# Expert gate and up weights: eight consecutive feature rows on a partition, and a gather that reads the normed rows with a stride of eight

## Chip, cores and metric

The kernel runs on one core of a Trainium2 chip. The metric is device time in microseconds (us), the median of several executions. A profile of one further execution gives the span from its first to its last instruction, the engines' busy times and the DMA packets. Engines are named as in the profile: PE (matrix multiply, with its weight loads as PEld), DVE (VectorE), ACT (ScalarE), POOL (GpSimd) and SP (SyncE, which here only issues DMAs; its queue is SPq).

## What is computed

A hybrid layer (attention, pooling mixer, gated feed-forward) is followed by two layers that each end in a mixture of experts. All is in 32-bit floats, on 256 tokens of 1024 features. The part that the change touches, per layer `l`:

```python
x = layer_norm(ALPHA * x + mix, ln1_g[l], ln1_b[l])
# grouped_moe: 16 experts, 4 groups, the 2 best experts of the best group per token
hg = jnp.einsum('nd,edf->nef', xt, w_gate)     # w_gate[l]: 16 x 1024 x 512
hu = jnp.einsum('nd,edf->nef', xt, w_up)       # w_up[l]:   16 x 1024 x 512
act = jax.nn.silu(hg) * hu * gates[:, :, None]
out = jnp.einsum('nef,efd->nd', act, w_down)   # w_down[l]: 16 x 512 x 1024
x = layer_norm(ALPHA * x + out, ln2_g[l], ln2_b[l])
```

## The kernel before, in words

Program order per engine is fixed when the kernel is built; engines wait for each other and for DMAs through semaphores. All weights are streamed from HBM by DMAs that SP issues in the order of the text, each as soon as the buffer that it fills is free.

**Attention part of a layer** (lines 802 to 1083): projections, index scores, two kinds of attention, output projection. Towards its end `ex.pump(12)` and `ex.pump(20)` let SP issue the first expert weights.

**Norm and routing** (lines 1085 to 1162): `z` is the normed row tile without scale and shift: tokens on partitions, features as 8 chunks of 128, in two halves `tt` of 128 tokens. `transpose_rows` turns `z` to features on partitions, and `affine` (line 1093) applies the layer norm's scale and shift, which lie per partition in `vec`. POOL splits `z` into `zh` and `zl` (lines 1128 to 1130), two reduced-precision floats that add up to it. The router then gives every token a slot (of 64) in each of its experts.

**Experts** (`routed_experts`, line 1265): 16 experts are taken as 8 pairs `p`. For every four experts `gather(q)` (line 1175) multiplies the rows with a 0/1 slot matrix `G`: for each feature chunk `k` and both halves, `zh` and `zl` are the stationary operand (128 x 128, loaded by a PEld instruction) and `G` the moving one (256 columns). That is 32 matmuls for each `q`, 4 gathers a layer, 256 matmuls in all. ACT (line 1096) or DVE (line 1098) applies `affine` and writes the chunk to `xg`. `gate_up(p, m)` (line 1191) multiplies 64 gathered slots per expert, as the stationary operand, with the gate (m = 0) or up (m = 1) weights: 8 chunks `k` for 2 experts `e`, which stand side by side in PE's columns. Then come silu and product, `slot_rows`, four transposes `pact` (line 1299; the stationary operand is `sg[:, k:512:4]`, every fourth column), `down` and `combine`, which adds the rows back to the tokens.

**Expert weights** (`Experts.pump`, line 722): gate and up weights of an expert come as two halves `h` of four 128-row chunks, `"(k p) f -> p k f"`: chunk `k` has feature row 128 k + p on partition p, so one partition's run in HBM is one row of 512 floats, 2 KB. Down weights come as `"(p k) f -> p k f"`: two rows of 1024 floats that are consecutive, 8 KB in one run. Pair 0's gate weights and the pairs 6 and 7 are loaded in smaller pieces (lines 728 to 738 and 754 to 759); the last pair's down weights in half rows, 2 KB (line 753). `KINDS` says which pool a piece's buffer is from; the pools are shared with activations.

The function `dense_experts` and the branch `need > 64` are a fallback for crowded experts that these inputs don't take.

Of the kernel before, what the change touches and what calls it, by code (L numbers as in the profile page):

```python
# [10 lines left out]
F32 = mybir.dt.float32  # L11
# [9 lines left out]
D = 1024  # L21
KD = D // 128
# [12 lines left out]
def body(tc, a, out, dbg=None, upto=None):  # L35
    nc = tc.nc
    te, ve, se, ge, sy = nc.tensor, nc.vector, nc.scalar, nc.gpsimd, nc.sync
    ctx = ExitStack()
    const = ctx.enter_context(tc.tile_pool(name="const", bufs=1))
# [5 lines left out]
    def A(name, shape=(128, 512)):  # L45

        return psum.tile(list(shape), F32, tag="A", name=name, bufs=4)

    def H(name, shape=(128, 2, 512)):

        return psum.tile(list(shape), F32, tag="H", name=name, bufs=2)

    def act(name, dt=F32, shape=(128, KD, T)):
        return wp.tile(list(shape), dt, tag="act", name=name, bufs=10)
# [18 lines left out]
    def mm(o, l, r, start, stop):  # L73
        return te.matmul(o, lhsT=l, rhs=r, start=start, stop=stop, skip_group_check=True)  # L74
# [26 lines left out]
    def keep_warm(n, dst):  # L101

        for _ in range(n):
            te.transpose(dst, ident, ident)
# [64 lines left out]
    for c in range(4):  # L169
        for u in range(4):  # L170
            if c == u == 0:
                t = W["in00"] = ring.tile([128, 2, 1024], F32, name="in00")
# [13 lines left out]
    for c in range(NF // 2):  # L186
        for s in range(2):
            c0 = s * DFF + 256 * c
# [64 lines left out]
    def V(n, j):  # L253
        b, o = VO[n]
        i = v0[b] + o + j
        if CV[0] <= i < CV[1]:
            return at.conv[:, i - CV[0]:i - CV[0] + 1]
        i -= CV[1] - CV[0] if i >= CV[1] else 0
        return vec[:, i:i + 1]

    def cload(name, shape, src, dt=F32, eng=None):
        t = const.tile(list(shape), dt, name=name)
        (eng or ge).dma_start(t, src)
        return t
# [19 lines left out]
    upb = cload("upb", (128, 2, 128), a["c_up"], BF16)  # L284
    cr = cload("cr", (128, 100), a["c_route"])
    iota64, tri, gsum = cr[:, 0:64], cr[:, 68:84], cr[:, 84:100]
    rbias = cload("rbias", (128, 16), a["router_bias_2"].partition_broadcast(128))

    rw = const.tile([128, (KD + 1) * 16], F32, name="rw")
# [368 lines left out]
    for i in range(NF):  # L658
        if True:
            ps = up_pair(i)  # L660
# [23 lines left out]
    ovf = const.tile([128, 2], F32, name="ovf")  # L684
    flag = const.tile([1, 1], I32, name="flag")
    m8 = const.tile([128, 2, 8], F32, name="m8")
    R = const.tile([128, 11, 32], F32, name="R")
    selb = const.tile([128, 2, 16], BF16, name="selb")
    gcol = const.tile([128, 8], F32, name="gcol")
    rn = const.tile([128, 4, 4], F32, name="rn")  # L690
# [21 lines left out]
    class Experts:  # L712
# [9 lines left out]
        def pump(self, n):  # L722
            while self.n < min(n, len(self.todo)):
                p, m, h, e = self.todo[self.n]
                shape = [128, 4, 512] if m < 2 else [128, 2, D]
                kind = KINDS[self.n]
                name = f"e{self.l}{p}{m}{h}{e}"
                if p == m == 0:

                    self.n += 2  # L730
                    for b in range(2):
                        for e in range(2):
                            t = ring.tile([128, 2, 512], F32, name=name)
                            c0 = 512 * h + 256 * b
                            sy.dma_start(t, a["w_gate_2"][self.l, e, c0:c0 + 256].rearrange("(k p) f -> p k f", p=128))
                            for k in range(2):
                                W[f"e{self.l}00{h}{e}", 2 * b + k] = t[:, k]
                    continue
                if kind == "r":
                    t = ring.tile(shape, F32, name=name)  # L740
                else:
                    t = dict(a=act, h=hl8, p=pp8)[kind](name, F32, shape)
                src = a[("w_gate_2", "w_up_2", "w_down_2")[m]][self.l, 2 * p + e]
                src = src.rearrange("(k p) f -> p k f" if m < 2 else "(p k) f -> p k f", p=128)[:, shape[1] * h:shape[1] * (h + 1)]
                if p < 6:
                    sy.dma_start(t, src)
                elif p == 7 and m == 2:

                    self.final.append((t, src))
                    if len(self.final) == 4:  # L750
                        for c in range(2):
                            for t_, s_ in self.final:
                                sy.dma_start(t_[:, :, 512 * c:512 * c + 512], s_[:, :, 512 * c:512 * c + 512])
                elif e:

                    for i in range(2):
                        s = slice(i * shape[1] // 2, (i + 1) * shape[1] // 2)
                        for t_, s_ in (self.last, (t, src)):
                            sy.dma_start(t_[:, s], s_[:, s])
                self.last = t, src  # L760
                for k in range(shape[1]):
                    W[name, k] = t[:, k]
                self.n += 1

    def transpose_rows(z, evac, one_bank):

        n = 2 if one_bank else 4
        pt = [A("pt", (128, 2, T)) if one_bank else H("pt", (128, 4, T)) for _ in range(KD // n)]
        if one_bank:
            keep_warm(36, pt[3][:, 1, 0:128])  # L770
        for tt, k in [(tt, k) for k in range(KD) for tt in range(2)] if one_bank else [(tt, k) for tt in range(2) for k in range(KD)]:
            if not one_bank and tt == 1 and k == 0:
                keep_warm(8, pt[1][:, 3, 128:])
            te.transpose(pt[k // n][:, k % n, tt * 128:(tt + 1) * 128], z(k, tt), ident)
        for k in range(KD):
            evac(k, pt[k // n][:, k % n])
# [22 lines left out]
    def layer(l, xT, xh, xl, general=False):  # L799
# [285 lines left out]
        z = act("z", shape=(128, 2, KD, 128))  # L1085
        zh, zl = act("zh", F32R, (128, 2, KD, 128)), act("zl", F32R, (128, 2, KD, 128))
# [3 lines left out]
                normalise(z[:, tt, 4 * c:4 * c + 4], acc[tt][c].rearrange("t (k p) -> t k p", p=128), mv, (se, ve)[c])  # L1090
        xp = act("xp")

        def affine(dst, src, k, eng):
            g, b = V(f"ln1g{l}", k), V(f"ln1b{l}", k)
            if eng is se:
                se.activation(dst, src, AF.Identity, scale=g, bias=b)
            else:
                ve.tensor_scalar(dst, src, g, b, op0=ALU.mult, op1=ALU.add)  # L1098

        transpose_rows(lambda k, tt: z[:, tt, k], lambda k, ps: affine(xp[:, k], ps, k, (se, ve)[k // 4]), False)  # L1100
        se.activation(warm[:, 0:1], xp[0:1, 3, 0:1], AF.Sigmoid)
        if dbg is not None and upto == f"xp{l}":
            sy.dma_start(dbg, xp)
# [19 lines left out]
        def rv(i):  # L1123
            return R[:, i].rearrange("p (t e) -> p t e", t=2)

# [5 lines left out]
        ve.tensor_tensor(out=bia, in0=aff, in1=rbias[:, None, :].to_broadcast([128, 2, 16]), op=ALU.add)  # L1131
        b4 = R[:, 1].rearrange("p (g e) -> p g e", e=4)
        cmp = t1("cmp", (128, 2, 8, 4, 4))
# [7 lines left out]
                             in1=tri[:, None, :].to_broadcast([128, n, 16]), op=ALU.is_gt)  # L1141
            ve.tensor_reduce(out=out, in_=o, axis=AX.X, op=ALU.add)

        rank, two = (R[:, i].rearrange("p (g e) -> p g e", e=4) for i in (10, 5))
        rank4(rank, b4, 8, 0)

        ve.scalar_tensor_tensor(out=two, in0=rank, scalar=1.5, in1=b4, op0=ALU.is_lt, op1=ALU.mult)
        q8 = [R[:, 9, 8 * i:8 * i + 8] for i in range(3)]
        ve.tensor_reduce(out=q8[0], in_=two, axis=AX.X, op=ALU.add)
        rank4(q8[1].rearrange("p (t g) -> p t g", t=2), q8[0].rearrange("p (t g) -> p t g", t=2), 2, 0)  # L1150
        ve.tensor_scalar(q8[2], q8[1], 0.5, None, op0=ALU.is_lt)
# [15 lines left out]
        def slots(q):  # L1167

            G = t2("G", (128, 2, 256), F32R)
            for tt in range(2):  # L1170
                ve.tensor_tensor(out=G[:, tt].rearrange("p (e s) -> p e s", s=64), in0=iota64[:, None, :].to_broadcast([128, 4, 64]),
                                 in1=sid[:, tt, 4 * q:4 * q + 4, None].to_broadcast([128, 4, 64]), op=ALU.is_equal)
            GS[q] = G

        def gather(q, bs=range(4)):

            G = GS[q]
            if q not in XG:
                XG[q] = act("xg", shape=(128, KD, 256))
            xg = XG[q]  # L1180
            for b in bs:
                pg = A("pg", (128, 2, 256))
                for tt in range(2):
                    for i in range(2):
                        k = 2 * b + i
                        mm(pg[:, i], zh[:, tt, k], G[:, tt], tt == i == 0, False)
                        mm(pg[:, i], zl[:, tt, k], G[:, tt], False, tt == 1)
                for i in range(2):
                    affine(xg[:, 2 * b + i], pg[:, i], 2 * b + i, (se, ve)[b % 2])

        def gate_up(p, m):
            ps = A("gu")
# [66 lines left out]
        def gates_():  # L1259
            ve.scalar_tensor_tensor(out=gat, in0=sid, scalar=0.5, in1=aff, op0=ALU.is_gt, op1=ALU.mult)  # L1260
            ve.tensor_reduce(out=R[:, 7, 2:4], in_=gat, axis=AX.X, op=ALU.add)
            ve.reciprocal(R[:, 7, 4:6], R[:, 7, 2:4])
            ve.scalar_tensor_tensor(out=gat, in0=gat, scalar=1 / ALPHA, in1=R[:, 7, 4:6, None].to_broadcast([128, 2, 16]), op0=ALU.mult, op1=ALU.mult)
# [88 lines left out]
        for tt in range(2):  # L1352
# [6 lines left out]
            for c in range(2):  # L1359
                s = slice(c * 512, c * 512 + 512)  # L1360
                v, g, b = z2[:, tt, s], gb[:, 0, s], gb[:, 1, s]
# [130 lines left out]
```

## Time and profile before

| | us |
|---|---|
| median of 3 executions (1076.24 to 1078.51) | 1077.11 |
| the profiled execution's own time | 1077.54 |
| its span, first to last instruction | 1075.8 |
| PE busy | 1026.4 (95%) |
| DVE busy | 540.2 (50%) |
| ACT busy | 428.1 (40%) |
| POOL busy | 88.6 (8%) |
| DMA, mean of 16 engines | 295.08 MB at 274 GB/s |

Busy times overlap, and a busy PE is not PE at its peak. The profiled execution's time is 1.7 us over its span and 0.4 us over the median of the others. The expert stages lie at 488 to 706 us (first of the two layers) and 844 to 1067 us (second).

### The profile page before, as it was taken

The page shows a single profiled execution, that of the slowest core. Times are in us where ns is not written, and L with a number is a line of the kernel's source. Part 1 is how long each engine was busy: PE and PEld are TensorE (multiplying, and loading weights), DVE is VectorE, ACT ScalarE, POOL GpSimd, SP SyncE. Part 2 cuts the span into 40 slices and gives each one's busy share as a digit, 9 for nine tenths or more (in the row PEclk, how much of TensorE's full clock was granted, in tenths as well). Part 3 has the DMA queues.
Part 4 walks back from the last instruction along what each step waited for, and adds up shares of the span by engine and source line. Part 5 has one row for each costly group of instructions (what it writes and reads, how often), then busy time and mean ns, then how long its engine had stood idle before and what let it go on. Part 6 is the DMA issues. An engine that isn't in the chain of part 4 may idle for free.

```text
span 1075.8 us, 16369 instructions
## 1 busy us (share of the span) xinstructions
PE 1026.4 (95%) x6620; PEld 729.0 (68%) x6620; DVE 540.2 (50%) x1022; ACT 428.1 (40%) x795; POOL 88.6 (8%) x88
## 2 busy tenths in 40 slices
PE   9999999999999999998999999989999899999995
PEld 7889999999999999764343434378976534343432
DVE  6775668977776789653010111058985302021103
ACT  5675548655554565541010111166654302011111
POOL 3400021000000120020000000043000200000001
PEclk9999999999999999999999999999999899999998
DMA  9943555755443254987999999964297899999994
GB/s 341 349 141 130 169 197 195 245 187 196 132 130 143 84 196 158 340 309 263 398 396 393 395 399 395 378 225 175 90 345 276 299 374 393 400 399 400 395 387 155
DMA packets 131636, 295.08 MB, mean 274 GB/s; under 512 B 6022, under 2 KB 34896, under 8 KB 125280
## 3 DMA queue, kind: packets, MB, share of 16 engines
q1 hardware_dynamic: 129936, 290.44, 73.5%
q0 software_dynamic: 1312, 2.97, 0.8%
q8 instruction: 54, 0.88, 0.3%
q10 hardware_dynamic: 304, 0.53, 0.1%
q14 instruction: 30, 0.25, 0.1%
HBM read 291.82 MB, written 2.10 MB: 273 GB/s over the span
## 4 chain that ended last, share of the span: by engine, by line
PE 75%; DVE 13%; DMA 6%; ACT 5%; issue 1%; SPq 0%; POOL 0%; ACTq 0%; DVEq 0%; POOLq 0%
PE gu L74 20%; PE up L74 12%; PE pd L74 8%; PE fm L74 7%; PE yT L74 5%; PE tm L74 4%; PE sc L74 4%; DVE hl L86 3%; PE prj L74 3%; PE pg L74 3%; PE wo L74 2%; PE sum L74 2%; DMA e<-in_w_up_dram 2%; DMA e<-in_w_down_dram 1%; ACT P L399 1%
## 5 line engine op out<-in xcount | busy, mean ns | idle before, releaser
L74 PE MATMUL gu<-e,xg 128*64 128x512 f32 x1024 | 228.1, 597 | 1.3 <-ACT sg L1284 1.3
L74 PEld LDWEIGHTS gu<-e,xg 128*64 128x64 f32 x1024 | 71.6, 138 | 135.4 <-issue 128.0
L74 PE MATMUL up<-h2h,hl 128*128 128x256 f32 x704 | 130.5, 283 | 0.0
L74 PE MATMUL pd<-e,aT 128*64 128x512 f32 x512 | 113.8, 596 | 2.4 <-ACT aT L1301 2.3
L74 PEld LDWEIGHTS up<-h2h,hl 128*128 128x128 f32 x704 | 111.4, 192 | 0.0
L74 PE MATMUL up<-h2l,hl 128*128 128x256 f32 x352 | 99.7, 283 | 0.1
L74 PEld LDWEIGHTS pd<-e,aT 128*64 128x64 f32 x512 | 35.2, 137 | 72.0 <-issue 64.7
L74 PEld LDWEIGHTS up<-h2l,hl 128*128 128x128 f32 x352 | 67.6, 192 | 0.3 <-DVE h2l L524 0.3
L1215 DVE TENSOR_REDUCE gcol<-pgt 64x1 f32<-64x2 f32 x32 | 5.0, 157 | 124.8 <-PE pgt L74 124.5
L1290 DVE SCALAR_TENSOR_TENSOR sg<-gu,gcol,sg 128x512 f32<-128x512 f32 x16 | 12.0, 751 | 110.1 <-PE gu L74 110.1
L74 PE MATMUL yT<-ac,hl 128*128 128x256 f32 x528 | 67.0, 283 | 0.1
L74 PEld LDWEIGHTS yT<-ac,hl 128*128 128x128 f32 x528 | 64.9, 192 | 0.3 <-ACT ac L644 0.3
L86 DVE TENSOR_TENSOR hl<-up,hl 128x1024 fp32r<-128x1024 f32 x44 | 53.8, 1225 | 19.5 <-ACT hl L96 19.4
L1284 ACT ACTIVATE sg<-gu 128x512 f32<-128x512 f32 x16 | 9.6, 598 | 128.0 <-PE gu L74 128.0
L96 ACT ACTIVATE hl<-up 128x1024 fp32r<-128x1024 f32 x44 | 46.1, 1051 | 33.9 <-PE up L74 28.4
L1316 ACT ACTIVATE y<-pd 128x512 fp32r<-128x512 f32 x32 | 18.5, 597 | 99.5 <-PE pd L74 80.7
L86 DVE TENSOR_TENSOR y<-pd,y 128x512 fp32r<-128x512 f32 x32 | 21.3, 686 | 66.4 <-ACT y L1316 66.4
L1301 ACT ACTIVATE aT<-pact 128x512 f32<-128x512 f32 x16 | 9.6, 599 | 110.4 <-PE pact L1299 110.4
L74 PE MATMUL fm<-hh,hl 128*128 128x256 f32 x256 | 49.2, 288 | 0.9 <-ACT vu L325 0.9
L1098 DVE TENSOR_SCALAR xg<-pg,vec 128x256 f32<-128x256 f32 x32 | 15.9, 538 | 61.2 <-PE pg L74 39.3
L86 DVE TENSOR_TENSOR hl<-in,hl 128x1024 fp32r<-128x1024 f32 x32 | 38.6, 1220 | 11.2 <-ACT hl L96 10.9
L74 PE MATMUL prj<-xhn,hl 128*128 128x256 f32 x208 | 40.3, 288 | 3.9 <-DVE iq L86 2.7
(357 smaller groups left out, 2073.2 us busy)
## 6 DMA issues: line engine op xcount, KB each, us to landing
e<-in_w_up_dram SPq DMA_DIRECT2D x48, 1024.0 KB, 14.1
e<-in_w_down_dram SPq DMA_DIRECT2D x48, 1024.0 KB, 13.6
e<-in_w_gate_dram SPq DMA_DIRECT2D x40, 1024.0 KB, 14.5
e<-in_w_gate_dram SPq DMA_DIRECT2D x48, 512.0 KB, 10.6
up<-in_w_up_dram SPq DMA_DIRECT2D x22, 1024.0 KB, 5.1
e<-in_w_up_dram SPq DMA_DIRECT2D x32, 512.0 KB, 10.8
e<-in_w_down_dram SPq DMA_DIRECT2D x32, 512.0 KB, 10.7
in<-in_w_in_dram SPq DMA_DIRECT2D x15, 1024.0 KB, 15.9
```

The costliest lines, as they stand in the source:

```text
L74: return te.matmul(o, lhsT=l, rhs=r, start=start, stop=stop, skip_group_check=True)
L86: return (eng or ve).tensor_tensor(out=dst, in0=src, in1=hi.bitcast(F32), op=ALU.subtract)
L96: se.activation(hi, raw, AF.Copy, scale=scale)
L399: se.activation(P[:, i, c:c + n], S[:, i, c:c + n], AF.Exp, scale=scale if isinstance(scale, float) else scale[:, tt:tt + 1], bias=m[:, 1, ...
L1098: ve.tensor_scalar(dst, src, g, b, op0=ALU.mult, op1=ALU.add)
L1215: ve.tensor_reduce(out=gcol[r, p:p + 1], in_=pt[r, x:x + 17:16], axis=AX.X, op=ALU.add)
L1284: se.activation(sg, psg, AF.Silu)
L1290: ve.scalar_tensor_tensor(out=sg, in0=psu, scalar=gcol[:, p:p + 1], in1=sg, op0=ALU.mult, op1=ALU.mult)
L1301: se.activation(aT, pt, AF.Copy)
L1316: se.activation(h_, pd[c], AF.Copy)
```

## The change

Feature row 8 p + k, in place of 128 k + p, now lies on partition p in chunk k, for gate and up weights alike. So four consecutive rows (8 KB) of one partition are one run in HBM; pieces of two rows are runs of 4 KB. The sum over features is the same in another order, and the gathered rows have to follow: `gather` takes every eighth feature from column k on as its stationary operand (a step of 32 bytes), and `affine` takes scale and shift from a new tile `lnp` that holds them in the same order, loaded by four small DMAs on POOL's queue early in the program. `R` shrinks by three planes, whose contents move to free ones. The down weights and the fallback stay.

```diff
+    lnp = const.tile([128, 2, 2, KD], F32, name="lnp")
+    for l in range(2):
+        for i, n in enumerate(("ln1_g_2", "ln1_b_2")):
+            ge.dma_start(lnp[:, l, i], a[n][l].rearrange("(p k) -> p k", k=KD))
...
-    R = const.tile([128, 11, 32], F32, name="R")
+    R = const.tile([128, 8, 32], F32, name="R")
...
-                            c0 = 512 * h + 256 * b
-                            sy.dma_start(t, a["w_gate_2"][self.l, e, c0:c0 + 256].rearrange("(k p) f -> p k f", p=128))
+                            src = a["w_gate_2"][self.l, e].rearrange("(p k) f -> p k f", p=128)
+                            sy.dma_start(t, src[:, 4 * h + 2 * b:4 * h + 2 * b + 2])
...
-                src = src.rearrange("(k p) f -> p k f" if m < 2 else "(p k) f -> p k f", p=128)[:, shape[1] * h:shape[1] * (h + 1)]
+                src = src.rearrange("(p k) f -> p k f", p=128)[:, shape[1] * h:shape[1] * (h + 1)]
...
-        def affine(dst, src, k, eng):
-            g, b = V(f"ln1g{l}", k), V(f"ln1b{l}", k)
+        def affine(dst, src, g, b, eng):
...
-        rank, two = (R[:, i].rearrange("p (g e) -> p g e", e=4) for i in (10, 5))
+        rank, two = (R[:, i].rearrange("p (g e) -> p g e", e=4) for i in (2, 5))
...
-        q8 = [R[:, 9, 8 * i:8 * i + 8] for i in range(3)]
+        q8 = [R[:, 6, 8 * i:8 * i + 8] for i in range(3)]
...
+            zf = [[v[:, tt].rearrange("p k c -> p (k c)") for v in (zh, zl)] for tt in range(2)]
...
-                        mm(pg[:, i], zh[:, tt, k], G[:, tt], tt == i == 0, False)
-                        mm(pg[:, i], zl[:, tt, k], G[:, tt], False, tt == 1)
+                        mm(pg[:, i], zf[tt][0][:, k:D:KD], G[:, tt], tt == i == 0, False)
+                        mm(pg[:, i], zf[tt][1][:, k:D:KD], G[:, tt], False, tt == 1)
...
-                    affine(xg[:, 2 * b + i], pg[:, i], 2 * b + i, (se, ve)[b % 2])
+                    k = 2 * b + i
+                    affine(xg[:, k], pg[:, i], lnp[:, l, 0, k:k + 1], lnp[:, l, 1, k:k + 1], (se, ve)[b % 2])
```

On PE, DVE, ACT and SP the instructions stand in the same order as before, with the same sizes. On POOL four DMAs are added, in the program's opening, between the routing constants and the router's bias. Before:

```order
L263 DMA upb<-in_c_up_dram 128x256
L263 DMA cr<-in_c_route_dram 128x100
L263 DMA rbias<-in_router_bias_dram 128x16
L291 DMA rw<-in_router_w_dram 128x8x16
L292 DMA rw<-in_router_w_dram 128x16
L363 TENSOR_TENSOR qk<-qk,bw 128x512 x4
```

and with the change (line numbers are five higher from there on):

```order
L263 DMA upb<-in_c_up_dram 128x256
L263 DMA cr<-in_c_route_dram 128x100
L291 DMA lnp<-in_ln_g_dram 128x8
L291 DMA lnp<-in_ln_b_dram 128x8
L291 DMA lnp<-in_ln_g_dram 128x8
L291 DMA lnp<-in_ln_b_dram 128x8
L263 DMA rbias<-in_router_bias_dram 128x16
L296 DMA rw<-in_router_w_dram 128x8x16
L297 DMA rw<-in_router_w_dram 128x16
L368 TENSOR_TENSOR qk<-qk,bw 128x512 x4
```

The bias and router loads, and the four multiplications of `qk` behind them on POOL, now stand behind the four new issues.

## Rows read from the trace of the kernel before

**Rows 1.** Windows of layer 0's expert stage; busy us (count) by engine, clock, DMA:
```profile
core 0: us, PE busy (x) PEld busy (x) DVE busy (x) ACT busy (x) POOL busy (x), PEclk, DMA share, GB/s
...
547.00:571.00 24.00, 24.00 (x114) 9.11 (x115) 2.82 (x7) 1.73 (x4) 0.00 (x0) 1.00 1.04 402
...
sum 218.00, PE 211.63 PEld 89.32 DVE 31.70 ACT 32.68 POOL 0.00; mean PE 23.51 PEld 9.92 DVE 3.52 ACT 3.63 POOL 0.00
```

**Rows 2.** Waits that a DMA ended; engine, line, in total us, times, longest:
```profile
DVE xg L1098 <- DMA e<-in_w_up_dram: 21.9, 2, 10.9
...
PEld gu L74 <- DMA e<-in_w_up_dram: 1.4, 5, 0.3
...
PEld gu L74 <- DMA e<-in_w_down_dram: 0.6, 2, 0.3
```

**Rows 3.** Timeline of DVE at two gathers (start us, us, engine, what):
```profile
598.62 0.99 DVE L1098 TENSOR_SCALAR xg<-pg,vec 128x256 f32<-128x256 f32 x2 [10.68 <-PE pg L74]
...
652.05 0.99 DVE L1098 TENSOR_SCALAR xg<-pg,vec 128x256 f32<-128x256 f32 x2 [10.93 <-DMA e<-in_w_up_dram]
```

**Rows 4.** End of layer 0's experts: SP's issues, landing time, then PE:
```profile
680.66 8.65 SPq L753 DMA_DIRECT2D e<-in_w_down_dram  x7
...
e<-in_w_down_dram SPq DMA_DIRECT2D x16, 512.0 KB, 10.6
...
696.19 5.37 PE L74 MATMUL pd<-e,aT 128*64 128x512 f32 x24
701.49 1.20 PE L74 MATMUL sum<-y,GT 128*128 128x512 f32 x4
702.62 1.94 PE L74 MATMUL pd<-e,aT 128*64 128x512 f32 x8
```

**Rows 5.** Windows with gate and up weights in flight, then with down weights:
```profile
544.00:557.00 13.00, 13.00 (x73) 6.38 (x73) 2.73 (x7) 3.02 (x6) 0.00 (x0) 1.00 1.05 385
561.50:570.00 8.50, 8.50 (x42) 3.92 (x42) 1.51 (x3) 0.60 (x1) 0.00 (x0) 1.00 1.01 410
```

**Rows 6.** SP's issues that belong to those windows:
```profile
538.11 10.33 SPq L746 DMA_DIRECT2D e<-in_w_up_dram  x4
550.66 4.24 SPq L746 DMA_DIRECT2D e<-in_w_down_dram  x4
```

**Rows 7.** The page's DMA packets, and issues with us to landing:
```profile
DMA packets 131636, 295.08 MB, mean 274 GB/s; under 512 B 6022, under 2 KB 34896, under 8 KB 125280
...
e<-in_w_up_dram SPq DMA_DIRECT2D x48, 1024.0 KB, 14.1
e<-in_w_down_dram SPq DMA_DIRECT2D x48, 1024.0 KB, 13.6
```

**Rows 8.** The gather's weight loads and matmuls, all of them (ns min/median/max):
```profile
L74 PEld LDWEIGHTS pg<-G,zh x128: 186/192/330, 488.1 to 1012.2; 128*128 128x128 f32 x128
L74 PE MATMUL pg<-G,zh x128: 278/283/553, 488.1 to 1012.4; 128*128 128x256 f32 x128
```

**Rows 9.** Two of the gather's weight loads on the timeline, four loads apart:
```profile
597.10 0.19 PEld L74 LDWEIGHTS pg<-G,zh 128*128 128x128 f32 x1
...
597.58 0.19 PEld L74 LDWEIGHTS pg<-G,zh 128*128 128x128 f32 x1
```

**Rows 10.** Other weight loads: strided transposes, contiguous transposes, 64 columns:
```profile
L1299 PEld LDWEIGHTS pact<-ident,sg x64: 195/209/221, 509.4 to 1052.6; 128*128 128x128 f32 x64
...
L774 PEld LDWEIGHTS pt<-ident,z x48: 138/141/143, 476.4 to 835.7; 128*128 128x128 f32 x48
...
L74 PEld LDWEIGHTS gu<-e,xg x1024: 132/137/231, 491.5 to 1050.1; 128*64 128x64 f32 x171
```

**Rows 11.** Strided transposes of one pair on the timeline, PE:
```profile
562.72 0.63 PE L1299 MATMUL pact<-ident,sg 128*128 128x128 f32 x4
```

**Rows 12.** POOL around its last opening DMAs:
```profile
34.42 0.55 POOL L292 DMA_DIRECT2D rw<-in_router_w_dram  x1
40.04 2.13 POOL L363 TENSOR_TENSOR qk<-qk,bw 128x512 f32<-128x512 f32 x1 [5.08 <-DVE qk L361]
```

More of the change, by code (lines that the diff above doesn't have):

```diff
@@ L1098, in affine @@
                 ve.tensor_scalar(dst, src, g, b, op0=ALU.mult, op1=ALU.add)
-        transpose_rows(lambda k, tt: z[:, tt, k], lambda k, ps: affine(xp[:, k], ps, k, (se, ve)[k // 4]), False)
+        transpose_rows(lambda k, tt: z[:, tt, k], lambda k, ps: affine(xp[:, k], ps, V(f"ln1g{l}", k), V(f"ln1b{l}", k), (se, ve)[k // 4]), False)
         se.activation(warm[:, 0:1], xp[0:1, 3, 0:1], AF.Sigmoid)
```

## Prediction

> **What bounds the kernel now.** I read the expert stages first, since every changed transfer and every changed matmul but the four loads in the opening belongs to them. Question one is whether PE waits for weights there. In the windows of layer 0's expert stage [rows 1] PE is busy 211.63 of 218.00 us, in one of them all 24.00 of 24.00, while DVE and ACT are busy some 32 us each and POOL not at all; so PE sets the pace. The 16 DMA engines are saturated at the same time (share 1.04, 402 GB/s), so the table alone doesn't say whether they hold PE up. Three further views do. In the list of waits [rows 2] a DMA ends waits of PE's weight loads for the experts for 1.4 and 0.6 us, none of them over 0.3 us. The long one, of DVE (21.9 us), is of an engine that idles anyway; and the half of it that ends at 652.05 us has a twin at 598.62 us, the same two instructions of the same 0.99 us, whose wait is put down to PE's gather [rows 3]: the landing only came at the same moment. Last, the end of the stage, where the DMA lead is smallest [rows 4]: the last of seven half-size pieces is issued before 689.3 us, such a piece lands 10.6 us after its issue, so it is there at about 699.6 us; the matmuls that need it start at 702.62 us, at the heels of the four `combine` matmuls (701.49 + 1.20 us). The weights are three microseconds early at the tightest place. PE is the bound; the DMAs are nearly one.
>
> **The change, part by part.**
>
> *Longer runs.* In a stretch in which gate and then up weights are in flight (the up weights are issued from 538.11 us on and take 14.1 us to land) the DMAs move 385 GB/s at a share of 1.05; where the down weights issued from 550.66 us on are (13.6 us to landing), 410 GB/s at 1.01 [rows 5 to 7]. The down pieces are the ones in 8 KB runs; only 131636 − 125280 = 6356 packets of the whole program are that large [rows 7]. So 1 MB (1.049 million bytes) takes 2.72 us in 2 KB runs and 2.56 us in 8 KB runs, 0.17 us less. A layer has 64 such pieces of gate and up weights: at most 10.6 us of DMA time per layer, less in truth, since 20 of them will come in 4 KB runs. What it is worth to the end: nothing, because PE isn't waiting for it; the lead of 3 us grows. Where SP is then ahead it meets buffers that PE has not yet freed. I take 0 us; the other end, all of it on the path, is −21 us.
>
> *The gather's strided operand.* This is the only part that PE itself feels. There are 256 such matmuls (128 for `zh` [rows 8], as many for `zl`), now at 0.12 us each: four steps from 597.10 to 597.58 us [rows 9]. Each step holds a load of 128 columns and a matmul of 256. The price of a 32-byte step isn't in the trace; the nearest row is the transpose `pact`, whose stationary operand has a 16-byte step [rows 10]. First the load's fixed part: 64 columns take 137 ns [rows 10], the gather's 128 take 192 [rows 8], so 64 columns are 55 ns, 128 are 110, and 82 ns are fixed. A contiguous transpose load (141 ns) is then 59 ns of reading, a strided one (209 ns) 127 ns, or 114 by its minimum of 195. Two readings are possible. Either a strided load reads a column in 0.9 to 1.0 ns whatever it is for; the gather's loads, with 110 ns for 128 columns, go at 0.86 ns already, and hardly change. Or a stride doubles what the load took before, and they go from 110 to about 220 ns.
>
> For the first reading speaks the step of the strided transposes: four of them take 0.63 us, so (0.63 − 0.28) / 3 = 0.116 us a step [rows 11], taking off the 283 ns of one matmul [rows 8], no more than the gather's 0.12. A load of that rate fits into the gather's step as it is. I take 0. Low end: 0, since no row shows a strided load faster than a contiguous one. If the 17 ns between 127 and 110 show, 256 × 17 ns = 4.4 us. High end: the load doubled, a step of 0.12 + 0.11 us, 256 × 0.11 = 28.2 us. All of it would be on the path, since PE has no idle time there to take it.
>
> The Trainium skill, page "SBUF — State Buffer", section "Door 1: The DMA port swizzle", says that SBUF has 16-byte lines, that two accesses are needed in one line for full rate, and that a stride up to four 32-bit elements is free. The trace agrees on the penalty and not on where it starts, since the step of four elements already costs (209 against 141 ns). By that rule the gather, with one access per line, would be slower, and the time would be the first rival's.
>
> *Four loads of `lnp`.* POOL issues them behind `cr`; one issue takes 0.55 us, and POOL then idles 5.08 us before it multiplies `qk` at 40.04 us [rows 12]. 2.2 us fit in; were that cover gone, `qk` would come late by what is over, a microsecond at most. 4 × 128 runs of 32 bytes are 16 KB beside 295 MB. 0 us.
>
> *Everything else.* The order on PE, DVE, ACT and SP is the same; `affine` reads its two scalars from another tile, in instructions of the same size; POOL writes `zh` and `zl` by whole halves before and after, so the gather waits for nothing new; the planes of `R` only move. 0 us.
>
> Sum: 1077.54 us of the profiled execution + 0 − 0. That execution is 0.4 us above the median of the others, so I say **1077.2 us**, no change. A difference under 0.2% (2.2 us) can't be told from none here.
>
> **Rivals.**
>
> *A strided load takes twice its time.* The place is each of the 256 gather steps, the price 0.11 us, and it decides as soon as the load (now 110 ns) outgrows the step of 120. For it: the strided transposes' reading is twice the contiguous one's, 127 or 114 against 59. Against it: their absolute rate, which is the gather's own. Time: 1077.1 + 28.2 = 1105.3 us, slower by 2.6%. Chance 0.25.
>
> *A stride adds a fixed amount.* By the same rows a stride adds 209 − 141 = 68 ns to a load of 128 columns. Added to the gather's loads, the step goes from 0.12 to 0.19 us, 256 × 0.068 = 17.4 us: 1094.5 us; by the minimum, 195 − 138 = 57 ns, 14.6 us: 1091.7. Chance 0.17.
>
> *The DMAs are the bound after all.* Saturation for whole stages speaks for it, as does a lead of only 3 us at the end, and the trace can't show a stall that is spread over many steps. Against it stand PE's 24.00 of 24.00 us and the list of waits. If half of the 10.6 us per layer reached the path, the time would be 1077.1 − 10.6 = 1066.5 us. Chance 0.06. That the transfers don't get faster is possible too, but as they are hidden it would leave my time where it is.
>
> **How the numbers follow.** My forecast has 0.52; of that 0.46 lies within 0.2% of 1077.1, 0.04 above (the 4.4 us) and 0.02 below. So faster is 0.06 + 0.02 = 0.08, the same 0.46, slower 0.25 + 0.17 + 0.04 = 0.46. The forecast's own range is 1075 to 1081.5 us. To leave out no more than 2 in 10 the range has to reach into the first rival: 1075 to 1105 us leaves out the DMA-bound case and about half of the doubled loads.
>
> **What would show it.** Right: the packets of 8 KB and more rise by ten thousands; gate and up stretches move about 410 GB/s; the last pieces land earlier than 699.6 us against the pair's matmuls; the gather's weight loads read 190 to 215 ns and four of its steps still take 0.48 us; the `down` matmuls start where they did. Wrong: weight loads of `pg` near 260 or 300 ns and steps of 0.19 or 0.23 us; a gather of 32 matmuls that takes 6 to 7 us of PE's time in place of 4; or PE idle times in the stage of before that vanish together with DMA time.

## Result and profile after

| | before | after |
|---|---|---|
| median of four executions, us | 1077.17 | 1109.15 (1107.20 to 1110.87) |
| ratio, with its 95% interval | | 1.0289 (1.0273 to 1.0304) |
| profiled execution / its span, us | 1077.54 / 1075.8 | 1107.20 / 1105.4 |
| PE busy, us | 1026.4 | 1055.1 |
| DMA packets | 131636 | 87732 |

The change makes the kernel 2.9% slower, 32 us. The two profiled executions, which the traces below show, differ by 29.7 us: the changed kernel's is the fastest of its four. The gather's loads and matmuls after the change, all of them (ns min/median/max, first and last start); they answer to [rows 8]:

```profile
L74 PEld LDWEIGHTS pg<-G,zh x128: 312/338/344, 489.1 to 1041.4; 128*128 128x128 f32 x128
L74 PE MATMUL pg<-G,zh x128: 385/409/609, 489.1 to 1041.6; 128*128 128x256 f32 x128
```

A load takes 338 ns in place of 192. Less the fixed 82 ns that the prediction read from the trace of before, 256 ns of reading stand in place of 110, 2.3 times as much. Five loads in a row on the timeline of PEld, beside [rows 9]:

```profile
604.24 0.34 PEld L74 LDWEIGHTS pg<-G,zh 128*128 128x128 f32 x1
604.48 0.34 PEld L74 LDWEIGHTS pg<-G,zl 128*128 128x128 f32 x1
604.72 0.34 PEld L74 LDWEIGHTS pg<-G,zh 128*128 128x128 f32 x1
604.96 0.34 PEld L74 LDWEIGHTS pg<-G,zl 128*128 128x128 f32 x1
605.20 0.34 PEld L74 LDWEIGHTS pg<-G,zh 128*128 128x128 f32 x1
```

Four steps take 0.96 us, 0.24 each, where four took 0.48. PEld is busy all the time in such a gather (columns as in [rows 1]; the first row is of the kernel before, the others of the changed one). It was so before, when loads of 192 ns overlapped, so this alone doesn't show that the load sets the step; experiment 4 asks that. The DMAs go on at full rate:

```profile
596.50:598.00 1.50, 1.50 (x13) 1.50 (x14) 0.00 (x0) 1.43 (x3) 0.00 (x0) 1.00 1.02 410
...
604.00:607.50 3.50, 3.50 (x15) 3.50 (x16) 0.00 (x0) 1.99 (x4) 0.00 (x0) 1.00 1.02 417
615.00:640.00 25.00, 24.78 (x118) 9.13 (x115) 3.12 (x7) 2.77 (x5) 0.00 (x0) 1.00 1.02 415
```

The DMA part did what it says: fewer and larger packets, shorter landings [rows 7], from the page:

```profile
DMA packets 87732, 295.09 MB, mean 267 GB/s; under 512 B 6150, under 2 KB 35024, under 8 KB 70112
...
e<-in_w_up_dram SPq DMA_DIRECT2D x48, 1024.0 KB, 10.2
e<-in_w_down_dram SPq DMA_DIRECT2D x48, 1024.0 KB, 9.0
```

87732 − 70112 = 17620 packets have 8 KB or more, where 6356 had.

**Where the time came from.** Gather 1 of the first layer is one unbroken row of 32 loads. From its first to its last load before took 542.95 to 546.65 us, 31 steps of 0.119; after takes 546.44 to 553.88, 31 steps of 0.240. Added up over the fourteen unbroken rows of `pg` loads, 31.1 us became 58.2; with the last step of each row (14 x 0.12 = 1.7 us) the gathers cost 28.8 us more. That is less than 256 x 0.121 = 31.0, because the first row of each layer was slow already: its steps took 0.187 and 0.211 us before, in stretches with a granted clock (the share of its full 2.4 GHz that PE is given) of 0.50. About another microsecond was lost at 50 us, in the opening (experiment 5). Between these places the two traces run in step but for two such stretches: one that only the changed kernel has, at 745.6 to 749.0 us, costs it 0.7 us, and one that before had at 843.5 to 850.3 us is half as long in the changed kernel, which gives back 0.9. Together that is some 29.6 us; the last four `combine` matmuls start 29.7 us later (1092.41 against 1062.73).

### The profile page after: what moved, and what is told of

Read it like the earlier page. It is cut to its first block, busy times and chain, and to the rows that moved or that the text cites. A ratio compares the mean times of both kernels' runs of the same rounds, so it can differ in the third digit from the quotient of the medians.

```text
span 1105.4 us, 16376 instructions
## 1 busy us (share of the span) xinstructions
PE 1055.1 (95%) x6620; PEld 758.2 (69%) x6620; DVE 540.3 (49%) x1022; ACT 428.4 (39%) x795; POOL 89.9 (8%) x92
## 2 busy tenths in 40 slices
DMA packets 87732, 295.09 MB, mean 267 GB/s; under 512 B 6150, under 2 KB 35024, under 8 KB 70112
## 4 chain that ended last, share of the span: by engine, by line
PE 75%; DVE 12%; ACT 5%; DMA 4%; issue 2%; POOL 1%; SPq 0%; DVEq 0%; ACTq 0%; POOLq 0%
PE gu L74 20%; PE up L74 11%; PE pd L74 10%; PE fm L74 7%; PE pg L74 6%; PE yT L74 5%; PE sc L74 4%; PE prj L74 3%; DVE hl L86 3%; PE sum L74 2%; PE wo L74 2%; DMA e<-in_w_gate_dram 1%; ACT hl L96 1%; ACT P L404 1%; PE sc L413 1%
## 5 line engine op out<-in xcount | busy, mean ns | idle before, releaser
L74 PE MATMUL pg<-G,zh 128*128 128x256 f32 x128 | 55.1, 430 | 5.1 <-DVE xg L1102 3.4
L1102 DVE TENSOR_SCALAR xg<-pg,lnp 128x256 f32<-128x256 f32 x32 | 15.9, 539 | 87.8 <-PE pg L74 87.8
L74 PE MATMUL pg<-G,zl 128*128 128x256 f32 x128 | 53.2, 416 | 0.0
L74 PEld LDWEIGHTS pg<-G,zh 128*128 128x128 f32 x128 | 43.0, 336 | 13.0 <-issue 8.3
## 6 DMA issues: line engine op xcount, KB each, us to landing
e<-in_w_up_dram SPq DMA_DIRECT2D x48, 1024.0 KB, 10.2
e<-in_w_up_dram SPq DMA_DIRECT2D x32, 512.0 KB, 10.2
e<-in_w_down_dram SPq DMA_DIRECT2D x32, 512.0 KB, 10.2
```

## Experiments

In experiments that read the gathered features in another order than the weights' rows, the time is that of the same instructions.

**1. The stride alone, and 2. the runs alone.** Kernel before with the strided operand, and the changed kernel without it:

```diff
 # 1: to the kernel before
+zf = [[v[:, tt].rearrange("p k c -> p (k c)") for v in (zh, zl)] for tt in range(2)]
-mm(pg[:, i], zh[:, tt, k], G[:, tt], tt == i == 0, False)
+mm(pg[:, i], zf[tt][0][:, k:D:KD], G[:, tt], tt == i == 0, False)
...
 # 2: to the changed kernel
-mm(pg[:, i], zf[tt][0][:, k:D:KD], G[:, tt], tt == i == 0, False)
+mm(pg[:, i], zh[:, tt, k], G[:, tt], tt == i == 0, False)
...
```

> The kernel before with one edit: the gather's stationary operand is read with the step of eight elements, from column k on. Weights, their DMAs, scale and shift stay as before, so the gathered features stand in another order than the weights' rows and the sums are of mismatched features. Theory (the strided weight load is the whole loss): the loads of pg read about 338 ns, the step 0.24 us in place of 0.12, 256 x 0.121 = 31 us, so about 1108 us, no less than the changed kernel's 1109. Rival (the loss comes from something else of the change, such as longer DMA writes that disturb PE's reads of the same memory): loads stay near 192 ns or rise by a part only, and the time stays near 1077 us.

> The changed kernel with one edit undone: the gather reads its stationary operand contiguously again, while the weights keep their 8 KB runs and lnp stays; features and weight rows are therefore mismatched in the sums. Theory (the DMA gain is real and hidden behind PE): 8 KB packets as in the changed kernel (over 17,000), landings near 10 us, loads of pg back at 192 ns, and 1076 to 1078 us. Rival (DMAs were a hidden bound before): 1056 to 1071 us, by 5 to 10 us a layer. Rival (longer runs cost PE something besides the stride): above 1080 us.

Measured: 1107.24 us with the stride alone, 1.0275 times before (1.0259 to 1.0290); 1079.18 us with the runs alone, 1.0011 times (1.0002 to 1.0020). The loads, in this order:

```profile
L74 PEld LDWEIGHTS pg<-G,zh x128: 312/338/344, 488.9 to 1041.4; 128*128 128x128 f32 x128
```

```profile
L74 PEld LDWEIGHTS pg<-G,zh x128: 186/192/330, 489.5 to 1014.2; 128*128 128x128 f32 x128
```

The stride makes the loss without any of the DMAs' changes, and without the stride all but 1.2 us of it is gone. These 1.2 us lie above the theory's 1076 to 1078 us; experiment 5 gives them to `lnp`. So longer runs neither disturb PE nor help it by more than about a microsecond. The transfers themselves did get better: with the runs alone the DMAs move 418 GB/s where they moved 385 [rows 5] (pieces of 1 MB land 11.5 to 12.8 us after their issue, not near 10 as expected). The last eight down pieces of layer 0 are issued by 681.3 us (671.75 + 9.54) and land 10.2 us after their issue, so some 12.6 us ahead of the matmuls that need them, where it was 3 us [rows 4]. PE has no use for the extra nine. Windows, SP's issues with their landing time, and PE of the kernel with the runs alone:

```profile
544.00:557.00 13.00, 13.00 (x77) 6.97 (x75) 3.21 (x8) 3.62 (x7) 0.00 (x0) 1.00 1.01 418
```

```profile
671.75 9.54 SPq L758 DMA_DIRECT2D e<-in_w_down_dram  x8
...
e<-in_w_down_dram SPq DMA_DIRECT2D x16, 512.0 KB, 10.2
```

```profile
704.15 1.94 PE L74 MATMUL pd<-e,aT 128*64 128x512 f32 x8
```

**3. How the price goes with the step.** Kernel before, steps of 2, 4 and 16 elements in place of 8:

```diff
+mm(pg[:, i], zf[tt][0][:, 128 * (k % 4):128 * (k % 4) + 256:2], G[:, tt], tt == i == 0, False)
...
+mm(pg[:, i], zf[tt][0][:, 64 * k:64 * k + 512:4], G[:, tt], tt == i == 0, False)
...
+zf = [v.rearrange("p t k c -> p (t k c)") for v in (zh, zl)]
+mm(pg[:, i], zf[0][:, 8 * tt + k:2 * D:16], G[:, tt], tt == i == 0, False)
```

> The kernel before with the gather's stationary operand read with a step of two elements (8 bytes); features and weight rows are mismatched in the sums. By the rule of 16-byte lines with two accesses in each (the Trainium skill, page SBUF - State Buffer, section Door 1: The DMA port swizzle) this step is free: loads of pg near 192 ns, a step of 0.12 us, about 1077 us. If any step above one costs, loads near 338 ns and about 1108 us. If the cost grows with the step, something between, such as 230 to 260 ns and 1080 to 1095 us.

> The kernel before with the gather's stationary operand read with a step of four elements (16 bytes); features and weight rows are mismatched in the sums. A step of two left the load at 195 ns, a step of eight made it 338. If the price is one of 16-byte lines (the Trainium skill, page SBUF - State Buffer, section Door 1: The DMA port swizzle, by its two accesses in a line), a step of four has one access in a line as the step of eight has: loads near 338 ns, steps of 0.24 us, about 1107 us. If the price grows with the step, or a step up to four is free (that page's second sentence on it), loads of 195 to 270 ns and 1077 to 1095 us.

> The kernel before with the gather's stationary operand read with a step of sixteen elements (64 bytes), over both token halves at once; tokens, features and weight rows are mismatched in the sums. If the price is that of one element in a 16-byte line, it is paid in full at the step of eight and a load stays at 338 ns: about 1107 us. If it grows with the step, loads are well over 400 ns, steps over 0.3 us, and the time is over 1120 us.

One execution each: 1076.78, 1106.72 and 1106.78 us. The loads of `zh` with steps of two, four and sixteen:

```profile
L74 PEld LDWEIGHTS pg<-G,zh x128: 193/195/330, 488.0 to 1011.4; 128*128 128x128 f32 x128
```

```profile
L74 PEld LDWEIGHTS pg<-G,zh x128: 308/329/333, 488.2 to 1041.0; 128*128 128x128 f32 x128
```

```profile
L74 PEld LDWEIGHTS pg<-G,zh x128: 291/316/333, 489.4 to 1040.5; 128*128 128x128 f32 x128
```

Two loads of the kernel with a step of four, four loads apart (0.95 us, 0.24 a step):

```profile
545.66 0.33 PEld L74 LDWEIGHTS pg<-G,zl 128*128 128x128 f32 x1
...
546.61 0.33 PEld L74 LDWEIGHTS pg<-G,zl 128*128 128x128 f32 x1
```

8 bytes cost 3 ns a load, 16 bytes nearly all of the price, and 64 bytes no more than 32 (a little less: 316 ns against 338, which no theory here explains). It is a price of two levels, with its edge between 8 and 16 bytes. Of the Trainium skill's two sentences ("SBUF — State Buffer", section "Door 1: The DMA port swizzle") the one on two accesses per 16-byte line fits all four steps; the one by which four elements of 32 bits are free doesn't, by 329 against 192 ns.

**4. What sets the step of 0.24 us.** The changed kernel, the `zl` matmuls half as wide:

```diff
-mm(pg[:, i], zf[tt][1][:, k:D:KD], G[:, tt], False, tt == 1)
+mm(pg[:, i, 0:128], zf[tt][1][:, k:D:KD], G[:, tt, 0:128], False, tt == 1)
```

> The changed kernel, in which the matmuls of zl (half of the gather's 256) have 128 moving columns in place of 256, so slots 128 to 255 miss the low part. It asks what sets the step of 0.241 us. If the load alone does, steps stay 0.241 us and the time 1107 us. If the load has to share its reads with the matmul that runs beside it, the steps that load zh (beside a short matmul) become shorter by up to 0.05 us: 128 x 0.05 = 6.4 us, 1101 us.

Measured, one execution: 1116.63 us, slower than the changed kernel, as neither theory expected. The loads answer the question all the same: they start every 0.24 us as before, beside wide and narrow matmuls alike, so the step is the load's. (From 547.99 to 549.20 us are five steps.)

```profile
547.99 0.34 PEld L74 LDWEIGHTS pg<-G,zl 128*128 128x128 f32 x1
548.23 0.34 PEld L74 LDWEIGHTS pg<-G,zh 128*128 128x128 f32 x1
...
549.20 0.34 PEld L74 LDWEIGHTS pg<-G,zh 128*128 128x128 f32 x1
```

That agrees with the Trainium skill ("TensorE: Matmul & The Clock Gate", section "Step-by-step: what each phase is for"), by which the stationary and the moving operand have read ports of their own. The extra time is the clock's: matched matmul by matmul with the changed kernel, the 9.4 us are lost in expert matmuls, in stretches where the granted clock is 0.50 (1.2 of 2.4 GHz). In this kernel it falls to that during the gather, in which every other matmul has half the columns, and the expert matmuls behind the gather begin at that clock: 32 of them take 8.07 us where they took 7.09. Windows (the seventh number column is the clock) and PE of this kernel, then PE of the changed kernel:

```profile
547.00:551.00 4.00, 4.00 (x17) 3.22 (x14) 1.20 (x2) 1.59 (x3) 0.00 (x0) 0.98 1.01 414
551.00:553.50 2.50, 2.50 (x12) 2.50 (x11) 0.99 (x2) 0.03 (x1) 0.00 (x0) 0.50 1.02 426
553.50:556.00 2.50, 2.50 (x12) 2.36 (x13) 0.21 (x1) 1.02 (x2) 0.00 (x0) 0.50 1.02 423
```

```profile
555.68 8.07 PE L74 MATMUL gu<-e,xg 128*64 128x512 f32 x32
```

```profile
554.35 7.09 PE L74 MATMUL gu<-e,xg 128*64 128x512 f32 x32
```

The changed kernel nearly escapes this price: in its own gather at 610 to 612 us the granted clock was 0.50 too, but the loads kept their 0.24 us, and the clock was back at 1.00 from 614 us on:

```profile
610.00:612.00 2.00, 2.00 (x10) 2.00 (x10) 0.15 (x1) 0.65 (x2) 0.00 (x0) 0.50 1.00 418
...
614.00:616.00 2.00, 2.00 (x12) 0.72 (x10) 0.19 (x1) 0.00 (x0) 0.00 (x0) 1.00 1.03 430
```

**5. The four loads of `lnp` alone.** Kernel before with them, and with the smaller `R`:

```diff
+    lnp = const.tile([128, 2, 2, KD], F32, name="lnp")
+    for l in range(2):
+        for i, n in enumerate(("ln1_g_2", "ln1_b_2")):
+            ge.dma_start(lnp[:, l, i], a[n][l].rearrange("(p k) -> p k", k=KD))
```

> The kernel before with only the four DMAs of lnp on POOL's queue and the smaller R added; nothing reads lnp, and the computation is the reference's. The kernel with the runs alone took 1.2 us more than before, and in its trace POOL waits for landings between these issues and starts on qk at 43.86 us in place of 40.04, after which PE waits 0.94 us for DVE near 50 us. Theory (the four issues cost that): 1078.5 to 1079.5 us, 1.2 to 1.6 us over before, with qk on POOL at 43 to 44 us. Rival (the 1.2 us come from the expert stages, as of longer runs): within 0.3 us of before.

Measured: 1078.94 us, 1.0010 times before (1.0001 to 1.0019): 1.1 us by this ratio and 1.5 by the medians, where experiment 2 had 1.2. POOL in this kernel:

```profile
34.32 0.54 POOL L291 DMA_DIRECT2D lnp<-in_ln_g_dram  x1
37.49 0.54 POOL L291 DMA_DIRECT2D lnp<-in_ln_b_dram  x1 [2.64 <-DMA at<-in_c_att_dram]
40.15 0.54 POOL L263 DMA_DIRECT2D rbias<-in_router_bias_dram  x1 [2.12 <-DMA bw<-in_c_band_dram]
41.87 0.90 POOL L296 DMA_DIRECT2D rw<-in_router_w_dram  x1 [1.19 <-DMA bw<-in_w_pool_dram]
42.76 0.55 POOL L297 DMA_DIRECT2D rw<-in_router_w_dram  x1
43.32 5.04 POOL L368 TENSOR_TENSOR qk<-qk,bw 128x512 f32<-128x512 f32 x4
```

The issues themselves fit, as predicted; the waits between them don't. Each of the three waits is for the landing of the DMA that was issued eight places earlier (`at`, `band` and `wpool`). The program asks for that, not the chip: its POOL DMAs take eight completion semaphores in turn (numbers 111 to 118 in the trace), and each issue waits until the last DMA on its own semaphore has landed. The kernel before has the same waits, one of them right ahead of `rbias`:

```profile
33.00 0.54 POOL L263 DMA_DIRECT2D rbias<-in_router_bias_dram  x1 [0.55 <-DMA rows<-in_ln_b_dram]
```

With `lnp`, `qk` starts at 43.32 in place of 40.04 us [rows 12], DVE rotates it late, and PE's `tm` matmuls at 50 us start a microsecond later than before, 0.6 us of which arise there (1.0 to 1.2 us in experiments 2 and 6 and in the changed kernel). This one trace loses another 1.5 us at 177 us, in 3.4 us at a granted clock of 0.50; experiment 1, which has no `lnp`, has the same stretch, so differences of a microsecond are better taken from the medians than from single traces. Put together, 1.0275 x 1.0010 = 1.0285, the changed kernel's 1.0289 within its interval.

**6. The reordering on POOL.** The changed kernel with a contiguous gather:

```diff
-ge.tensor_copy(zh[:, tt], z[:, tt])
-lo_of(zl[:, tt], z[:, tt], zh[:, tt], ge)
+zp = z[:, tt].rearrange("t k p -> t (k p)").rearrange("t (p k) -> t k p", k=KD)
+ge.tensor_copy(zh[:, tt], zp)
+lo_of(zl[:, tt], zp, zh[:, tt], ge)
...
-mm(pg[:, i], zf[tt][0][:, k:D:KD], G[:, tt], tt == i == 0, False)
+mm(pg[:, i], zh[:, tt, k], G[:, tt], tt == i == 0, False)
```

> The changed kernel, but POOL does the reordering: it writes zh and zl in the order of the weights' rows, reading z with the step of eight in the two copies and two subtractions that it does anyway, and the gather reads contiguously. The computation is the reference's. In the changed kernel's place POOL ends its split 3.6 us ahead of the gather. Theory (the stride costs only where PE has no idle time): the gather's loads are back at 192 ns, and the time is 1076 to 1078 us, as long as POOL's strided reads add under 3.6 us to a layer's split of 5.7 us. If they double it, POOL ends some 2 us late in each layer, and the time is 1079 to 1083 us. Rival (the changed kernel loses by its DMAs): about 1109 us.

Measured: 1084.35 us, 1.0056 times before (1.0042 to 1.0070). 25 us come back, but 6 stay, more than expected; some 1.2 of them are `lnp`'s (experiment 5). The slack of 3.6 us was misread: it is not the gather that waits for POOL first but DVE's routing. POOL and DVE in this kernel:

```profile
484.21 5.67 POOL L86 TENSOR_TENSOR zl<-z,zh 128x1024 fp32r<-128x1024 f32 x2
```

```profile
487.32 2.62 DVE L1136 TENSOR_TENSOR R<-R,rbias 128x32 f32<-128x32 f32 x1 [0.94 <-ACT R L1131]
```

An addition of 32 columns lasts 2.62 us, until 489.94; POOL ends at 489.88. Before, the same addition took 0.60 us and ended with POOL as well, at 484.4:

```profile
483.85 0.60 DVE L1131 TENSOR_TENSOR R<-R,rbias 128x32 f32<-128x32 f32 x1 [0.94 <-ACT R L1127]
```

This agrees with the Trainium skill ("SBUF — State Buffer", section "Who interferes with whom"): a DVE instruction with two inputs from SBUF and a reading POOL instruction exclude each other. So each layer loses two microseconds of routing, and some more at the norm ahead of it (POOL's cast takes 2.06 us in place of 1.04).

**7. How near the DMAs are.** Kernel before with shorter runs in pairs 1 to 5:

```diff
-if p < 6:
+if 0 < p < 6 and m < 2:
+    for c in (0, 256):
+        sy.dma_start(t[:, :, c:c + 256], src[:, :, c:c + 256])
+elif p < 6:
```

> The kernel before with shorter runs: the gate and up weights of pairs 1 to 5 are loaded in two DMAs of 256 columns each, runs of 1 KB in place of 2 KB. The computation is the reference's. It asks how far the DMAs are from being the bound. Their lead at the tightest place was 3 us. If packets of 1 KB take 8 to 12% more DMA time, the 40 pieces of a layer cost some 9 to 13 us of it, more than the lead: PE would wait 5 to 10 us in each layer, 1087 to 1097 us. If the lead is larger than read, 1076 to 1080 us. Either way it bounds what longer runs are worth as cover.

Measured: 1089.50 us, 1.0109 times before (1.0094 to 1.0125). Waits of PE's loads that a DMA ended, in total us, times, longest; beside [rows 2]:

```profile
PEld gu L74 <- DMA e<-in_w_up_dram: 9.3, 14, 1.2
PEld gu L74 <- DMA e<-in_w_gate_dram: 3.5, 6, 1.2
```

The DMA engines, as busy as before [rows 5], move less, 349 GB/s in place of 385 or 10% more time for a piece, as expected; so it is the transfers that are slow, not SP's issues:

```profile
544.00:557.00 13.00, 13.00 (x77) 7.13 (x77) 2.99 (x7) 3.62 (x7) 0.00 (x0) 1.00 1.09 349
```

So the kernel before did stand at the edge: runs of half the length show on PE, 4.6 us in layer 0 and 6.3 us in layer 1, where it waits for the last pair's weights. Those are loaded as before, but stand in line behind the slower pieces. Runs of four times the length show nowhere, since the edge was on the good side already.

**8. A milder order.** Two consecutive rows on a partition (runs of 4 KB, a step of two in the gather), `lnp` loaded behind the multiplications of `qk`:

```diff
-src = src.rearrange("(p k) f -> p k f", p=128)[:, shape[1] * h:shape[1] * (h + 1)]
+src = src.rearrange(*(["(g p i) f -> p g (i f)"] if m < 2 else ["(p g i) f -> p g (i f)"]), p=128, i=(2, 2, 1)[m])[:, 2 * h:2 * h + 2]
...
-mm(pg[:, i], zf[tt][0][:, k:D:KD], G[:, tt], tt == i == 0, False)
+mm(pg[:, i], zf[tt][0][:, 256 * (k // 2) + k % 2:256 * (k // 2) + 256:2], G[:, tt], tt == i == 0, False)
```

> The changed kernel with a milder order: feature row 256 g + 2 p + i on partition p in chunk 2 g + i, so runs are 4 KB, the gather's stationary operand has a step of two, and lnp (in the same order) is loaded by POOL behind the multiplications of qk. The computation is the reference's. Theory (a step of two is nearly free, 195 against 192 ns; lnp cost only by standing ahead of qk; the DMA gain is hidden): 1076.5 to 1078.5 us, the same as before. Rival (the new order itself costs): above 1080 us. Rival (DMA gain): below 1075 us.

Measured: 1078.82 us, 1.0009 times before (1.0001 to 1.0018). 30 us better than the changed kernel, and nothing gained on the kernel before: it lies 0.3 us above the theory's range, and a microsecond seems to stay, whose cause is open. In the profiled execution PE loses nothing at 50 us any more; 1.7 us arise at 512 us, in 3.4 us at a granted clock of 0.50 that the trace of before doesn't have there, and 0.9 of them are made good at 849 us. No version here beats the kernel before, and with PE as the bound longer runs give it nothing to win.

## Why the prediction was wrong

- *What bounds the kernel*: right. PE is the bound and the DMAs are nearly one (experiments 2 and 7).
- *Longer runs*, 0 us: right in the gain per transfer (418 GB/s where it read 410, experiment 2) and, within a microsecond, in its worth.
- *The gather's strided operand*, 0 us: this is the step that failed. Of its two readings the prediction chose "a strided load reads a column in 0.9 to 1.0 ns whatever it is for", because four strided transposes keep a step of 0.116 us [rows 11]. That took the absolute rate of another kind of load for a limit that holds for every load. The runs showed a step of 0.24 us in place of 0.12: with the transposes' own 16 bytes the gather's load costs 329 ns where theirs costs 209, and its step is 0.24 us (experiment 3), twice their 0.116. What comes near is the ratio: the transposes' reading grew from 59 to 127 ns, 2.2 times, the gather's from 110 to 256, 2.3 times. That the fixed 82 ns hold for the transposes too is an assumption of the prediction which no run here checks, so the agreement is a hint and no rule. The gather's contiguous load was slower than theirs to begin with (192 against 141 ns), a sign in [rows 8, 10] that the two don't share a rate. Why they differ stays open; a narrower matmul beside the load doesn't change it (experiment 4).
- *The first rival*, the load doubled: its mechanism was the right one, and its time of 1105.3 us 4 us short. Its step was 0.23 us and is 0.24, which makes 28.8 us in place of 28.2, since not every step paid in full; the rest is `lnp` (1.1 to 1.5 us) and what the executions differ by. It had a chance of 0.25, and the range ended at 1105 us, on purpose short of its upper half. The fixed amount of the second rival (57 to 68 ns) is refuted by 146 ns.
- *Four loads of `lnp`*, 0 us: wrong by 1.1 to 1.5 us. The prediction counted the issues (2.2 us against 5.08 us of idle time [rows 12]) and not the waits that four more DMAs ahead of `rbias` and `rw` would bring, of which the trace of before had shown one (0.55 us, experiment 5). It did allow a microsecond.
- *Everything else*, 0 us: right; the other stretches run in step but for the two named under the result, which nearly cancel.

## What to carry over

A stationary operand's stride is paid in the weight load, and where loads stand close behind each other it is PE's time: of 128 columns of 32 bits, a step of 8 bytes was free, and one of 16 to 64 bytes made reading 2.1 to 2.3 times as long. A rate that was read from one kind of load (0.116 us a step in the transposes) did not hold for another (0.24 in the gather); before carrying one over, see whether the two agree where both are contiguous. Before making transfers better, ask whether anything waits for them, and put the reordering that they need where an engine really idles, counting who else is held up by it.

## What was not expected of the hardware

- The price of a strided load has two levels and isn't proportional to the step: 195, 329, 338 and 316 ns at 8, 16, 32 and 64 bytes.
- A limit that looks like the chip's can be the program's: POOL's issues wait 2.64, 2.12 and 1.19 us in experiment 5 because eight semaphores are used in turn.
- Less work for PE can cost time: with narrower matmuls between slow loads the mean granted clock was 0.969 in place of 0.985, and the kernel took 1116.63 us where the changed kernel's profiled execution took 1107.20.
- A small addition on DVE with two inputs from SBUF is held to the end of a POOL instruction (2.62 us in place of 0.60).
